# Sum of reciprocals over rows of 1024: loads of eight rows, chains of four, and a new split of additions and products

## The chip, the cores and the metric

The kernel runs on one core of a Trainium2 chip. The metric is the device time of one execution in microseconds (us), as a median of several runs. Beside it stands the profile of one execution: its span, from the first to the last instruction, and what each engine did in it. The engines are TensorE (PE in the profile), VectorE (DVE), ScalarE (ACT), GpSimd (POOL) and SyncE (SP), which here only issues transfers. There are also 16 DMA engines, which move the input from HBM into the on-chip memory SBUF. PSUM is a second, smaller on-chip memory, into which TensorE writes its results.

## The reference

```python
def setup_inputs():
    batch, seq, dim = 32, 512, 1024
    return {"x": np.abs(np.random.randn(batch, seq, dim)).astype(np.float32) + 1e-6}

def reference(x):
    return np.sum(1.0 / x, axis=-1).astype(np.float32)
```

The input is 67.1 MB, the output 64 KB. Every one of the 16384 rows of 1024 numbers becomes one number, the sum of its reciprocals.

## The kernel before

Each of the 128 partitions holds 128 rows of the input, so "a row" below means 128 x 1024 numbers, one row for each partition: 512 KB of input. The kernel goes through the 128 rows in 67 groups of one or two rows, in the list `GROUPS` (L39).

The arithmetic rests on 1/a + 1/b = (a + b) / (a b). A row is cut into halves a and b of 512 numbers (`H`). The product a b is needed for 512 places only, its reciprocal is taken by ACT as exp(-ln(S a b)) in two passes (`Ln`, L106, and `Exp`, L111), and DVE then multiplies with a + b and adds up the row, in one instruction with an accumulator (`tensor_tensor_reduce`, L118).

A group goes through these steps:

- SP issues its load (L83) into a tile `xt` of a pool with 16 buffers.
- POOL makes the products `pr` of its rows (L85); in the very last group DVE does.
- Where the group is marked `on_pe` (class B), TensorE adds the two halves of a row into a PSUM tile `sm`, as two matmuls with the identity matrix (L90). Each of these shows as two passes in the profile.
- ACT does `Ln` and `Exp` of the products. Without TensorE (class A) `Exp` writes to the PSUM tile `rc`, and with TensorE it writes back into `pr`.
- DVE sums the row. In class A it goes through all 1024 numbers of the row, each half against the same 512 reciprocals (`rc`); in class B through 512, `pr` against `sm`. In the profile the first is CUSTOM_DVE_ANT_1, the second CUSTOM_DVE_ANT_0, and a short read of the accumulator follows each.
- Class C has one row like class A and one that ACT does alone: `Ln` and `Exp` of all 1024 numbers with ACT's own accumulator (L98, L99).

The cycle is A, B, A, B, C, B, A, B, sixteen rows less one for POOL, seven times; then five groups of two rows, and six of one row. Each engine works through its instructions in the order of its queue and waits at each for what it needs. SP holds a load back until its buffer is free. At the end one transfer (L131) writes the sums out.

Of the kernel before, what the change touches and what calls it, by code (L numbers as in the profile page):

```python
# [1 line left out]

# [6 lines left out]


@with_exitstack
def kernel(
    ctx: ExitStack,
    tc: tile.TileContext,
    x: bass.AP,
    out: bass.AP,
):

    nc = tc.nc
    f32 = mybir.dt.float32
    P = 128
    D = 1024
    H = D // 2  # L30
    F = 128

    S = float(2**17)

    GP, DV = nc.gpsimd, nc.vector
    A, B, C = (2, 0, GP, False), (2, 0, GP, True), (1, 1, GP, False)
    GROUPS = (  # L39
        [A, B, A, B, C, B, A, B] * 7  # L40
        + [A, B, A, B, A]
        + [(1, 0, GP, True), (1, 0, GP, False)] * 2
        + [(1, 0, GP, True), (1, 0, DV, True)]
    )

    Ln = mybir.ActivationFunctionType.Ln
    Exp = mybir.ActivationFunctionType.Exp
    mult = mybir.AluOpType.mult
    add = mybir.AluOpType.add

    x_v = x.flatten_outer_dims().rearrange("(p f) d -> p f d", p=P)
    out_v = out.flatten().rearrange("(p f) -> p f", p=P)

    act_sets = list(get_activation_tables(nc.m.arch).keys())
    nc.scalar.add_instruction(  # L55
        mybir.InstLoadActFuncSet(
            name=nc.get_next_instruction_name(),
            act_func_set_id=act_sets.index("natural_log_exp_and_others"),
            ins=[],
            outs=[],  # L60
        )
    )

    xpool = ctx.enter_context(tc.tile_pool(name="xpool", bufs=16))
    ppool = ctx.enter_context(tc.tile_pool(name="ppool", bufs=4))
    opool = ctx.enter_context(tc.tile_pool(name="opool", bufs=1))
    rpool = ctx.enter_context(
        tc.tile_pool(name="rpool", bufs=2, space=bass.MemoryType.PSUM)
    )

    spool = ctx.enter_context(
        tc.tile_pool(name="spool", bufs=2, space=bass.MemoryType.PSUM)
    )

    sums = opool.tile([P, F], f32)
    ident = opool.tile([P, P], f32)
    make_identity(nc, ident)

    c0 = 0
    for np_, ns, eng, on_pe in GROUPS:  # L80
        n = np_ + ns
        xt = xpool.tile([P, n, D], f32, tag="xt")
        nc.sync.dma_start(out=xt, in_=x_v[:, c0 : c0 + n, :])  # L83
        pr = ppool.tile([P, np_, H], f32, tag="pr")
        eng.tensor_tensor(out=pr, in0=xt[:, :np_, :H], in1=xt[:, :np_, H:], op=mult)  # L85
        if on_pe:
            sm = spool.tile([P, np_, H], f32, tag="sm")
            for j in range(np_):
                for h in range(2):
                    nc.tensor.matmul(  # L90
                        sm[:, j, :],
                        lhsT=ident,
                        rhs=xt[:, j, h * H : (h + 1) * H],
                        start=h == 0,
                        stop=h == 1,
                    )
        for j in range(np_, n):
            nc.scalar.activation(out=xt[:, j, :], in_=xt[:, j, :], func=Ln)  # L98
            nc.scalar.activation(  # L99
                out=xt[:, j, :],  # L100
                in_=xt[:, j, :],
                func=Exp,
                scale=-1.0,
                accum_out=sums[:, c0 + j : c0 + j + 1],
            )
        nc.scalar.activation(out=pr, in_=pr, func=Ln, scale=S)  # L106
        if on_pe:
            rc = pr
        else:
            rc = rpool.tile([P, np_, H], f32, tag="rc")  # L110
        nc.scalar.activation(out=rc, in_=pr, func=Exp, scale=-1.0)  # L111
        for j in range(np_):
            if on_pe:
                row, rec = rc[:, j, :], sm[:, j, :]
            else:
                row = xt[:, j, :].rearrange("p (h e) -> p h e", h=2)
                rec = rc[:, j, :].unsqueeze(1).to_broadcast([P, 2, H])
            nc.vector.tensor_tensor_reduce(  # L118
                out=row,
                in0=row,  # L120
                in1=rec,
                scale=S,
                scalar=0.0,
                op0=mult,
                op1=add,
                accum_out=sums[:, c0 + j : c0 + j + 1],
            )
        c0 += n
    assert c0 == F, c0

    nc.sync.dma_start(out=out_v, in_=sums)  # L131


# [1 line left out]
_INS = ['x']  # L135
_OUTS = [((32, 512), 'float32')]


# [23 lines left out]
```

## Time and profile before

| | |
|---|---|
| median of 11 runs | 174.62 us (174.52 to 175.33) |
| profiled execution | 174.58 us, span 172.4 us |
| POOL busy | 143.4 us (83%) |
| ACT busy | 142.0 us (82%) |
| TensorE busy | 121.0 us (70%) |
| DVE busy | 109.8 us (64%) |
| DMA | 67.18 MB in the input queue, 390 GB/s over the span |

Times are microseconds from the start of the span. A busy share is an average over the whole span, so it doesn't say which engine sets the end; for that the stretches of time and the chain of waits are needed. In the groups of instructions, each row gives the source line, the engine, the operation and its tiles, how many there were, their busy time, the mean of one in ns, and behind the second bar how long the engine had stood idle before them and what ended that. "x" before a number counts instructions.

### The profile page before, as it was taken

What the parts mean: (1) busy time and instruction counts of PE and PEld (TensorE: products, weight loads), DVE (VectorE), ACT (ScalarE), POOL (GpSimd) and SP (SyncE); (2) the same over time, 40 slices, a digit from 0 to 9 for tenths busy, and PEclk for the clock granted to TensorE, in tenths of its full rate; (3) what the DMA queues carried; (4) which work ended last, traced back from release to release, by engine and by line L of the source; (5) the groups of instructions that cost most, each with busy time, mean ns of one, the idle gap of its engine ahead of it and who ended that gap; (6) DMA issues with size and microseconds to landing.
All of it is one profiled execution on the core that took longest, in us unless ns stands there. A gap on an engine that the chain in (4) does not pass through costs nothing.

```text
span 172.4 us, 1342 instructions
## 1 busy us (share of the span) xinstructions
PE 121.0 (70%) x256; PEld 47.4 (27%) x256; DVE 109.8 (64%) x243; ACT 142.0 (82%) x156; POOL 143.4 (83%) x72
## 2 busy tenths in 40 slices
PE   0099766666877667788676668976677877679480
PEld 0033322222332222233322223422222332223130
DVE  0009757874757757775578847577577755788791
ACT  2169989899878998889888997889888898988981
POOL 1698799969899799987999688996999879999920
PEclk9999999999999999999999996999999999999999
DMA  5999999999999999999999999999999999999500
GB/s 196 428 428 426 422 422 414 424 426 424 416 424 424 420 418 422 424 424 418 424 422 422 418 418 420 426 418 420 424 422 420 420 424 424 422 413 407 225 0 15
DMA packets 9799, 67.25 MB, mean 390 GB/s; under 512 B 1088, under 2 KB 1216, under 8 KB 1984
## 3 DMA queue, kind: packets, MB, share of 16 engines
q1 hardware_dynamic: 9792, 67.18, 94.0%
q8 instruction: 2, 0.03, 0.1%
q14 instruction: 5, 0.04, 0.1%
HBM read 67.11 MB, written 0.07 MB: 390 GB/s over the span
## 4 chain that ended last, share of the span: by engine, by line
DMA 78%; POOL 11%; ACT 2%; issue 2%; DVE 2%; SPq 2%; PE 1%; POOLq 0%; DVEq 0%
DMA xt<-in_x_dram 78%; POOL pr L85 11%; SPq L83 2%; ACT pr L106 1%; PE sm L90 1%; DVE xt L118 1%; ACT rc L111 1%; DVE pr L118 0%; ACT pr L111 0%; DVE pr L85 0%; POOLq L85 0%; DVE sums L118 0%; DVEq L118 0%; DVEq L157 0%
## 5 line engine op out<-in xcount | busy, mean ns | idle before, releaser
L85 POOL TENSOR_TENSOR pr<-xt 128x1024 f32<-128x1024 f32 (+1 forms) x66 | 142.7, 2167 | 20.8 <-DMA xt<-in_x_dram 16.5
L90 PE MATMUL sm<-xt,ident 128*128 128x512 f32 x256 | 121.0, 617 | 46.8 <-DMA xt<-in_x_dram 44.8
L118 DVE CUSTOM_DVE_ANT_1 xt<-xt,rc 128x1024 f32<-128x1024 f32 x57 | 67.7, 1218 | 50.3 <-issue 25.9
L106 ACT ACTIVATE pr<-pr 128x1024 f32<-128x1024 f32 (+1 forms) x67 | 65.0, 970 | 24.2 <-POOL pr L85 23.2
L90 PEld LDWEIGHTS sm<-xt,ident 128*128 128x128 f32 x256 | 47.4, 195 | 119.5 <-issue 62.0
L118 DVE CUSTOM_DVE_ANT_0 pr<-pr,sm 128x512 f32<-128x512 f32 x64 | 41.6, 685 | 9.5 <-ACT pr L111 8.2
L111 ACT ACTIVATE pr<-pr 128x1024 f32<-128x1024 f32 (+1 forms) x34 | 34.2, 1006 | 1.0
L111 ACT ACTIVATE rc<-pr 128x1024 f32<-128x1024 f32 (+1 forms) x33 | 29.9, 906 | 0.8
L118 DVE DVE_READ_ACCUMULATOR2_ANT sums<- 128x1 f32 x121 | 10.0, 82 | 0.0
L99 ACT ACTIVATE xt<-xt 128x1024 f32<-128x1024 f32 x7 | 7.3, 1041 | 0.0
L98 ACT ACTIVATE xt<-xt 128x1024 f32<-128x1024 f32 x7 | 7.3, 1040 | 0.0
L55 ACT ACT_TABLE_LOAD x1 | 1.3, 1283 | 0.7 <-PEq L146 0.7
L99 ACT ACTIVATION_READ_ACCUMULATOR xt<-xt 128x1 f32 x7 | 1.3, 187 | 0.0
L85 DVE TENSOR_TENSOR pr<-xt 128x512 f32<-128x512 f32 x1 | 0.7, 684 | 0.0
masks.py:197 POOL MEMSET ident<- 128x128 f32 x1 | 0.2, 205 | 0.3 <-POOLq L146 0.3
masks.py:199 POOL TENSOR_SCALAR_AFFINE_SELECT ident<-ident 128x128 f32<-128x128 f32 x1 | 0.3, 294 | 0.1
L146 POOL MEMSET const-float32-0.0<- 128x1 f32 x1 | 0.1, 99 | 0.2 <-issue 0.2
L146 POOL MEMSET const-bfloat16-1.0<- 128x1 bf16 x1 | 0.1, 102 | 0.0
L146 POOL MEMSET const-uint8-127<- 128x1 uint8 x1 | 0.1, 102 | 0.0
L146 POOL MEMSET const-float32-1.0<- 128x1 f32 x1 | 0.1, 99 | 0.0
## 6 DMA issues: line engine op xcount, KB each, us to landing
xt<-in_x_dram SPq DMA_DIRECT2D x61, 1024.0 KB, 19.8
xt<-in_x_dram SPq DMA_DIRECT2D x6, 512.0 KB, 15.6
out_dram<-sums SPq DMA_DIRECT2D x1, 64.0 KB, 1.5
```

Source lines behind the costliest of these rows:

```text
L55: nc.scalar.add_instruction(mybir.InstLoadActFuncSet(name=nc.get_next_instruction_name(), act_func_set_id=act_sets.index("natural_log_exp_ ...
L83: nc.sync.dma_start(out=xt, in_=x_v[:, c0 : c0 + n, :])
L85: eng.tensor_tensor(out=pr, in0=xt[:, :np_, :H], in1=xt[:, :np_, H:], op=mult)
L90: nc.tensor.matmul(sm[:, j, :], lhsT=ident, rhs=xt[:, j, h * H : (h + 1) * H], start=h == 0, stop=h == 1,)
L98: nc.scalar.activation(out=xt[:, j, :], in_=xt[:, j, :], func=Ln)
L99: nc.scalar.activation(out=xt[:, j, :], in_=xt[:, j, :], func=Exp, scale=-1.0, accum_out=sums[:, c0 + j : c0 + j + 1],)
L106: nc.scalar.activation(out=pr, in_=pr, func=Ln, scale=S)
L111: nc.scalar.activation(out=rc, in_=pr, func=Exp, scale=-1.0)
L118: nc.vector.tensor_tensor_reduce(out=row, in0=row, in1=rec, scale=S, scalar=0.0, op0=mult, op1=add, accum_out=sums[:, c0 + j : c0 + j + 1],)
L146: nc = _bacc.Bacc("TRN2", target_bir_lowering=False, num_devices=1)
```

## The change

The groups give way to 22 loads (`LOADS`): twelve of eight rows, then of 7, 6, 5, 4, 3, 2, 2, 1, 1 and 1. A load holds one or two chains of at most four rows, each given as (m, e, v): m rows, of which TensorE adds the halves of the first e, and DVE makes the products of the first v. An eight-row load is (4, 2, 0) and (4, 2, 1).

- A load of more than three rows uses one of four buffers of eight rows; the six small ones at the end have a buffer each (`epool`).
- POOL makes the products of up to four rows in one instruction. ACT takes `Ln` of a whole chain in one instruction, then `Exp` of the rows without TensorE into `rc` (two PSUM buffers), then `Exp` of the rows with TensorE in place. No row is done by ACT alone any more.
- TensorE writes each of its sums into a PSUM buffer of its own, of which there are four (before: two, of two rows each).
- For a row of which DVE makes the product, TensorE first copies half b into PSUM; DVE multiplies half a from SBUF with that copy; then TensorE adds half a. Only the last row (`DIRECT`) is multiplied from SBUF alone.
- DVE's sums of a chain (`sum_rows`) are put behind the products of the next chain (`waiting`). `keep` fixes the order of the loads, of POOL's and DVE's instructions and of the matmuls as written.

```diff
-    xpool = ctx.enter_context(tc.tile_pool(name="xpool", bufs=16))
+    xpool = ctx.enter_context(tc.tile_pool(name="xpool", bufs=4))
+    epool = ctx.enter_context(tc.tile_pool(name="epool", bufs=1))
...
+    LOADS = (
+        [[(4, 2, 0), (4, 2, 1)]] * 12
+        + [[(4, 2, 0), (3, 1, 1)], [(3, 1, 0), (3, 2, 1)], [(3, 1, 0), (2, 1, 1)]]
+        + [[(4, 2, 1)], [(3, 2, 1)], [(2, 1, 0)], [(2, 1, 1)]]
+        + [[(1, 0, 0)], [(1, 0, 0)], [(1, 1, 1)]]
+    )
+    DIRECT = 127
...
+    def add_half(s, half, start):
+        i = nc.tensor.matmul(
+            s, lhsT=ident, rhs=half, start=start, stop=True, skip_group_check=True
+        )
+        keep(i)
...
+    def sum_rows(c, xc, pr, sm, rc):
+        m, e = xc.shape[1], len(sm)
+        for j in range(e, m):
+            row = xc[:, j, :].rearrange("p (h e) -> p h e", h=2)
+            sum_row(c + j, row, rc[:, j - e, :].unsqueeze(1).to_broadcast([P, 2, H]))
+        for j in range(e):
+            sum_row(c + j, pr[:, j, :], sm[j])
...
+        for m, e, v in chunks:
+            xc = xt[:, q : q + m, :]
+            a, b = xc[:, :, :H], xc[:, :, H:]
+            pr = ppool.tile([P, m, H], f32, tag="pr")
+            sm = [spool.tile([P, H], f32, tag="s", name="s") for _ in range(e)]
+            if v < m:
+                keep(
+                    nc.gpsimd.tensor_tensor(
+                        out=pr[:, v:, :], in0=a[:, v:, :], in1=b[:, v:, :], op=mult
+                    )
+                )
+            for j in range(e):
+                add_half(sm[j], b[:, j, :], True)
+                if j >= v:
+                    add_half(sm[j], a[:, j, :], False)
+            for j in range(v):
+                other = b[:, j, :] if c0 + q + j >= DIRECT else sm[j]
+                keep(
+                    nc.vector.tensor_tensor(
+                        out=pr[:, j, :], in0=a[:, j, :], in1=other, op=mult
+                    )
+                )
+            for j in range(v):
+                add_half(sm[j], a[:, j, :], False)
+            if waiting:
+                sum_rows(*waiting)
+            nc.scalar.activation(out=pr, in_=pr, func=Ln, scale=S)
+            rc = None
+            if e < m:
+                rc = rpool.tile([P, m - e, H], f32, tag="rc")
+                nc.scalar.activation(out=rc, in_=pr[:, e:, :], func=Exp, scale=-1.0)
+            if e:
+                r = pr[:, :e, :]
+                nc.scalar.activation(out=r, in_=r, func=Exp, scale=-1.0)
+            waiting = c0 + q, xc, pr, sm, rc
+            q += m
```

`sum_row` is the same `tensor_tensor_reduce` as before, kept in order.

More of the change, by code (lines that the diff above doesn't have):

```diff
@@ L33 @@
     S = float(2**17)
[L37 to L43, printed above, removed]
+    LOADS = (
+        [[(4, 2, 0), (4, 2, 1)]] * 12
[3 rows of a table added]
     )
+    DIRECT = 127
     Ln = mybir.ActivationFunctionType.Ln
@@ L62 @@
     )
-    xpool = ctx.enter_context(tc.tile_pool(name="xpool", bufs=16))
+    xpool = ctx.enter_context(tc.tile_pool(name="xpool", bufs=4))
+    epool = ctx.enter_context(tc.tile_pool(name="epool", bufs=1))
     ppool = ctx.enter_context(tc.tile_pool(name="ppool", bufs=4))
     opool = ctx.enter_context(tc.tile_pool(name="opool", bufs=1))
+    spool = ctx.enter_context(
+        tc.tile_pool(name="spool", bufs=4, space=bass.MemoryType.PSUM)
+    )
     rpool = ctx.enter_context(
         tc.tile_pool(name="rpool", bufs=2, space=bass.MemoryType.PSUM)
-    )
-    spool = ctx.enter_context(
-        tc.tile_pool(name="spool", bufs=2, space=bass.MemoryType.PSUM)
     )
@@ L77 @@
     make_identity(nc, ident)
-    c0 = 0
[L80 to L95, printed above, removed]
-                    )
[L97 to L127, printed above, removed]
@@ new lines, with sum_row @@
+    keep = tc.keep_in_program_order
+    def add_half(s, half, start):
[3 more added lines that the diff above has]
+        keep(i)
+    def sum_row(c, row, fac):
+        i = nc.vector.tensor_tensor_reduce(
+            out=row,
+            in0=row,
+            in1=fac,
+            scale=S,
+            scalar=0.0,
+            op0=mult,
+            op1=add,
+            accum_out=sums[:, c : c + 1],
+        )
+        keep(i)
@@ new lines, in sum_rows @@
+    def sum_rows(c, xc, pr, sm, rc):
[5 more added lines that the diff above has]
+            sum_row(c + j, pr[:, j, :], sm[j])
+    waiting = None
+    c0 = 0
+    for k, chunks in enumerate(LOADS):
+        n = sum(m for m, _, _ in chunks)
+        if n > 3:
+            xt = xpool.tile([P, n, D], f32, tag="xt")
+        else:
+            xt = epool.tile([P, n, D], f32, tag=f"x{k}")
+        keep(nc.sync.dma_start(out=xt, in_=x_v[:, c0 : c0 + n, :]))
+        q = 0
+        for m, e, v in chunks:
[7 more added lines that the diff above has]
+                        out=pr[:, v:, :], in0=a[:, v:, :], in1=b[:, v:, :], op=mult
+                    )
+                )
[24 more added lines that the diff above has]
+            q += m
@@ L128 @@
         c0 += n
     assert c0 == F, c0
+    sum_rows(*waiting)
     nc.sync.dma_start(out=out_v, in_=sums)
```

## The prediction, made before the result was known

> **What bounds the kernel now.** The 40 slices come first (one character or number for 4.31 us).
>
> ```profile
> ACT  2169989899878998889888997889888898988981
> POOL 1698799969899799987999688996999879999920
> ...
> DMA  5999999999999999999999999999999999999500
> GB/s 196 428 428 426 422 422 414 424 426 424 416 424 424 420 418 422 424 424 418 424 422 422 418 418 420 426 418 420 424 422 420 420 424 424 422 413 407 225 0 15
> ```
>
> The DMA engines are full until about 160 us; then they stop while ACT and POOL go on. So the span is a full transfer plus a tail. The chain of waits, in order of time (start, us, what), shows where the tail is made:
>
> ```profile
> 118.98 19.81 DMA xt<-in_x_dram
> ...
> 138.95 2.35 POOL pr L85
> ...
> 156.29 2.39 POOL pr L85
> ...
> 158.70 1.06 ACT pr L106
> ...
> 168.85 0.69 DVE pr L118
> ```
>
> The chain follows DMA to 138.79, then POOL without a gap to 158.68, and only for the last 11 us a mixture of all engines. From 138.95 the timeline counts eight two-row and five one-row products on POOL, and DVE makes one: 22 rows, of which the first two landed at 138.79. So that was row 106 + 2 = 108 of 128. The first two had landed at 5.65 (POOL's first product begins at 5.75, after a wait for DMA). The **landing pace** is (138.79 - 5.65) / 106 = 1.256 us a row, which puts the last row at 138.79 + 20 x 1.256 = 163.9. The last sum ends at 169.55, the span at 172.4: 2.85 us for the output and the end.
>
> The groups by line and shape give prices (busy, mean ns of one | idle before):
>
> ```profile
> L85 POOL TENSOR_TENSOR pr<-xt 128x1024 f32<-128x1024 f32 x54 | 127.6, 2364 | 19.7 <-DMA xt<-in_x_dram 16.0
> L118 DVE CUSTOM_DVE_ANT_1 xt<-xt,rc 128x1024 f32<-128x1024 f32 x57 | 67.7, 1218 | 50.3 <-issue 25.9 <-ACT rc L111 12.7 <-POOL pr L85 11.8
> L118 DVE CUSTOM_DVE_ANT_0 pr<-pr,sm 128x512 f32<-128x512 f32 x64 | 41.6, 685 | 9.5 <-ACT pr L111 8.2
> ...
> L85 POOL TENSOR_TENSOR pr<-xt 128x512 f32<-128x512 f32 x12 | 15.2, 1278 | 1.1 <-DMA xt<-in_x_dram 0.6
> ```
>
> POOL: two rows 2.364, one 1.278, so 0.19 + 1.086 a row. A DVE sum from ACT's PSUM (ANT_1) and one with TensorE's sum (ANT_0) follow each other in the timeline every 1.145 and 0.605 us, the accumulator's read hidden. For ACT I take starts, since back-to-back instructions overlap (timeline of ACT):
>
> ```profile
> 158.70 1.06 ACT L106 ACTIVATE pr<-pr 128x1024 f32<-128x1024 f32 x1 [0.34 <-POOL pr L85]
> 159.79 1.03 ACT L111 ACTIVATE rc<-pr 128x1024 f32<-128x1024 f32 x1
> 160.75 0.61 ACT L106 ACTIVATE pr<-pr 128x512 f32<-128x512 f32 x1
> 161.40 0.63 ACT L111 ACTIVATE pr<-pr 128x512 f32<-128x512 f32 x1
> 161.93 0.61 ACT L106 ACTIVATE pr<-pr 128x512 f32<-128x512 f32 x1
> ```
>
> An Ln is followed by its own Exp after 1.09 us (two rows) or 0.65 (one); an Exp by the next instruction after 0.96 or 0.53. So Ln costs 0.21 + 0.44 a row, Exp 0.11 + 0.425 a row. From the same timeline: a POOL product reaches ACT after 0.03 us, an Exp in PSUM reaches DVE after 0.13, a DVE product reaches ACT after 0.04. DVE's one product of before (both inputs in SBUF) holds it for 0.61; with an input in PSUM, which no row shows, I take the same, as ANT_0 with such operands needs 0.605.
>
> [...] The four-row Ln, 2048 elements, no row shows; [...] The trace shows that: after a 2.13 us gap before 104.01 (columns: window, length, busy and count, granted clock, DMA share, GB/s)
>
> ```profile
> 101.00:104.00 3.00, 0.88 (x3) 1.00 1.03 421
> ...
> 105.00:106.00 1.00, 1.00 (x2) 0.50 1.05 442
> 106.00:107.00 1.00, 1.00 (x2) 0.50 1.01 418
> ...
> 109.00:110.00 1.00, 1.00 (x3) 1.00 1.03 426
> ```
>
> the passes took 0.85 us instead of 0.43.
>
> **The change, part by part.**
>
> *Loads of eight rows.* The same 67.1 MB come at, I assume, the same pace: 2-row loads already ran at 414 to 428 GB/s with 8 KB pieces. Larger pieces could gain something (rival 3). The first load lands at 5.65 + 6 x 1.256 = 13.2, 7.5 us later than now. What hides that: POOL's remaining work is 109 rows, 109 x 1.086 + 36 instructions x 0.28 (start and gap) = 128 us, and ends by 142 if unhindered; the transfers last until 163.9. Four 8-row buffers: in steady state a load is done 15.3 us after landing (POOL 4.67, ACT 3.89 twice, DVE's last sums 2.8), while the three behind it need 3 x 10.05 = 30.1 us to land. So SP has 15 us for reissuing, and the queue doesn't run dry. SP issues 22 loads instead of 67, at about 0.33 us each: nothing, behind full DMA.
>
> *Engines per eight rows (10.05 us of landing).* POOL 4 + 3 rows: 4.53 + 3.45 + 0.2 = 8.2, from 9.3 (a sixteen-row cycle of before: seven pairs and one single, 18.6). ACT 2 x (1.97 + 0.96 + 0.96) = 7.8. DVE 4 x 1.145 + 4 x 0.605 + one product 0.61 = 7.6. TensorE 8 x 0.86 = 6.9 at full clock. All are below 10.05: the first 96 rows cost nothing, whatever is removed there. ACT's own rows of class C go too, for the same reason free.
>
> *The tail.* The 7-row load lands at row 103: 138.79 - 5 x 1.256 = 132.5. POOL's four rows are done at 132.5 + 0.14 + 4.53 = 137.2, when ACT has long finished the load before (136.2). From there ACT has thirteen chains left, and smaller chains cost more a row: (4 rows) 3.89 twice, (3) 1.53 + 0.96 + 0.53 = 3.03 five times, (2) 1.09 + 2 x 0.53 = 2.16 three times, (1) 0.65 + 0.53 = 1.18 three times: **33.0 us**. Were there no gap, ACT would end at 170.2; that is already after now (168.82).
>
> *DVE's products.* Every product waits for TensorE's copy of half a row into PSUM (0.86 us); behind it in DVE's queue stand the previous chain's sums, ahead of it those of the one before that. ACT's Ln waits for it, and TensorE's second half, with the next chain's matmuls queued behind. In steady state it is ready 2.8 us before POOL's part. In the tail DVE is late. Following the thirteen chains with the prices above (start = the latest of engine, landing, predecessor, PSUM and pr buffers):
>
> ```
> rows left  chain    POOL done  product  ACT from-to      sums done
> 25         4 rows   137.2      -        137.2-141.1      143.9
> 22         3, v1    139.6      140.4    141.1-144.1      146.8
> 19         3        143.6      -        144.1-147.1      150.3
> 16         3, v1    146.1      147.4    147.5-150.5      152.7
> 13         3        149.9      -        150.5-153.5      156.2
> 11         2, v1    151.3      153.3    153.5-155.7      158.6
> 7          4, v1    154.9      156.8    156.8-160.7      163.6
> 4          3, v1    157.6      159.5    160.7-163.7      165.9
> 2 and 0:
>            2        160.1      -        163.7-165.9      168.4
>            2, v1    161.6      166.6    166.6-168.8      170.3
>            1        164.9      -        168.8-170.0      171.5
>            1        167.3      -        170.0-171.2      173.2
>            1, v1    -          172.1    172.1-173.3      174.1
> ```
>
> The gaps in ACT: 0.32 + 1.16 + 0.73 + 0.92 = **3.1 us**. Each arises alike: for the 4-row chain the sums of two chains earlier end at 156.2, the product takes 0.61, while ACT was free at 155.7. The last product multiplies straight from SBUF, but waits in DVE's queue all the same. POOL's late starts at the end (a pr buffer four chains back) end before ACT needs them. So: 170.2 + 3.1 + last sum and read 0.8 = 174.1; + 2.85 = span **176.9**. The profiled execution took 174.58 for a span of 172.4, 2.18 outside: 176.9 + 2.18 = **179.1 us**, 2.6% over the median of 174.62 (which the profiled one matches). Ends for what isn't shown: the gaps 0 to 5 us, the landing pace -3% to +1% of 132 us (-4 to +1)[...].
>
> **Rivals.** *1: products in time.* If DVE's sums are shorter or the order kinder, no gaps: 179.1 - 3.1 = 176.0. For: DVE is busy only 64% now. Against: the table, where ACT and DVE run neck and neck. *2: TensorE at half clock.* Eight rows leave it idle for 10.05 - 6.9 = 3.1 us a load, mostly in one piece, longer than the 2.13 that slowed it once. A slowed pass costs 0.43 more, four to eight such passes 1.7 to 3.4 us; in steady state ACT's 2.3 us of slack per load covers one, but in the tail PSUM sums and products come later by it: gaps grow by 1 to 3, 180 to 182. Against: TensorE becomes steadier busy when slowed. *3, on the faster side: pieces of 32 KB lift the transfer.* [...] It decides from 101 x d = 4.5 us, a pace of 1.211 (433 GB/s). Against: no 4.3 us slice of the profile exceeds 428. *4: the queue runs dry*, if a load is released more than 15 us later than I have it; each us late delays a landing by one, so 5 us late gives 184. I see nothing that would do it.
>
> **How the numbers follow.** The table's case 0.57, rival 1 0.15, rival 2 0.17, rival 3 0.08 (three quarters of it beyond parity), rival 4 0.03. A measurement of this kernel tells about 0.2% from no change (0.35 us). Rival 3 gives faster 0.06 and part of same 0.03; the rest, 0.91, is slower. The likeliest is 179.1, its own range 177.5 to 180.5. The range takes in rivals 1 and 2: 175.6 to 181.8, leaving out rivals 3 and 4 and the ends of 2.
>
> **What would show it.** Right: DMA still ends near 163.5; ACT nearly without gaps from 137 on, its waits there for DVE products, and the last Exp near 173; POOL done well before ACT. First wait of POOL about 13 us. Wrong: DMA well above 424 GB/s (rival 3), DMA gaps (4), TensorE at 0.5 clock in the tail (2), ACT's tail in one piece (1), or four-row Ln far from 1.9 us.

## The result, and the profile after

The changed kernel takes **176.97 us** (median of 13 runs, 175.9 to 177.95) beside 174.73 us for the kernel before: a ratio of 1.0105, with a 95% interval of 1.0087 to 1.0123, so it is slower. The runs of the kernel before fall into two groups, near 174.6 and near 175.4, and its median lies in the lower one; the quotient of the means (176.79 and 174.95) is 1.0105, that of the medians 1.013. The profiled execution took 176.01 us with a span of 174.2, so it is one of the shorter ones. Times here and below are those of undisturbed executions: one of e2 (179.34 us) and one of the kernel before (691.18 us, in the group of e5 to e8) are left out.

The 40 slices of the changed kernel (one of 4.36 us each):

```profile
DVE  0000396783989696987949698786959899998993
ACT  2000884957797795959498695959598998979962
POOL 1009859595978959594987959595989999795500
...
DMA  6999999999999999999999999999999999995000
GB/s 218 429 436 391 429 429 436 436 436 429 429 438 429 436 421 436 444 418 414 429 436 438 406 459 414 446 429 410 434 436 438 409 426 410 421 411 236 0 0 15
```

DMA moves more in most slices than the 414 to 428 GB/s of before, and stops some 2.6 us earlier (36.5 slices of 4.36 us against 37.5 of 4.31). ACT and POOL now show a hole in every load, and DVE, which was the least busy of the three before, is nearly full through the last ten.

POOL's timeline shows where loads land, since POOL waits for each of them (start, us, what, idle before and what ended it):

```profile
13.36 7.91 POOL L126 TENSOR_TENSOR pr<-xt 128x2048 f32<-128x2048 f32 x2 [12.06 <-DMA xt<-in_x_dram]
...
43.34 8.00 POOL L126 TENSOR_TENSOR pr<-xt 128x2048 f32<-128x2048 f32 x2 [1.77 <-DMA xt<-in_x_dram]
53.05 7.96 POOL L126 TENSOR_TENSOR pr<-xt 128x2048 f32<-128x2048 f32 x2 [1.71 <-DMA xt<-in_x_dram]
...
130.23 6.90 POOL L126 TENSOR_TENSOR pr<-xt 128x2048 f32<-128x2048 f32 x2 [0.54 <-DMA xt<-in_x_dram]
```

Two eight-row loads follow each other at 53.05 - 43.34 = 9.71 us, 1.214 us a row. The seven-row load lets POOL start at 130.23; the forecast had it land at 132.5. From the first load (row 8) to this one (row 103) the mean pace is (130.23 - 13.36) / 95 = 1.230 us a row, where the forecast had 1.256.

ACT's timeline of the last 32 rows, only those Ln that had to wait:

```profile
134.83 1.91 ACT L145 ACTIVATE pr<-pr 128x2048 f32<-128x2048 f32 x1 [0.75 <-POOL pr L126]
...
145.22 1.48 ACT L145 ACTIVATE pr<-pr 128x1536 f32<-128x1536 f32 x1 [0.48 <-DVE pr L137]
...
154.56 1.91 ACT L145 ACTIVATE pr<-pr 128x2048 f32<-128x2048 f32 x1 [1.14 <-DVE pr L137]
...
164.30 1.06 ACT L145 ACTIVATE pr<-pr 128x1024 f32<-128x1024 f32 x1 [0.17 <-DVE pr L137]
...
169.75 0.63 ACT L145 ACTIVATE pr<-pr 128x512 f32<-128x512 f32 x1 [1.54 <-DVE pr L137]
```

ACT begins the tail at 134.83 and then has gaps of 0.48, 1.14, 0.17 and 1.54 us, all waiting for a product of DVE. And the windows of the tail (engine busy, with the number of instructions: PE, PEld, DVE, ACT, POOL; then granted clock, DMA share, GB/s):

```profile
134.00:146.00 12.00, 9.91 (x22) 3.65 (x21) 11.39 (x25) 10.68 (x11) 11.31 (x5) 1.00 1.00 424
146.00:158.00 12.00, 10.12 (x23) 3.85 (x22) 11.23 (x26) 10.73 (x12) 10.55 (x5) 1.00 0.99 412
158.00:172.00 14.00, 6.79 (x15) 2.30 (x13) 13.44 (x30) 11.18 (x16) 3.84 (x3) 0.94 0.10 39
```

DVE, the third of them, is busy 11.39 + 11.23 + 13.44 = 36.1 of 38 us; ACT only 32.6, with the same list of work as in the forecast. In the same windows of the kernel before DVE had 26.0:

```profile
134.00:146.00 12.00, 9.42 (x21) 3.85 (x22) 7.09 (x18) 11.19 (x13) 10.44 (x5) 1.00 1.01 421
146.00:158.00 12.00, 9.30 (x21) 3.55 (x20) 9.39 (x19) 10.15 (x10) 11.44 (x6) 1.00 1.01 416
158.00:172.00 14.00, 7.22 (x16) 2.41 (x14) 9.49 (x23) 9.49 (x15) 6.82 (x6) 1.00 0.30 117
```

The chain of waits, in order of time:

```profile
112.04 4.53 POOL pr L126
116.58 1.92 ACT pr L145
118.53 1.04 ACT rc L149
...
122.73 6.21 PE s L83 x10
128.97 0.36 DVE pr L137
...
149.76 0.60 DVE pr L89
...
150.37 0.43 DVE pr L137
...
169.75 0.64 ACT pr L145
170.41 0.64 ACT pr L152
171.07 0.69 DVE pr L89
```

It leaves the transfer at 112 us and passes POOL and ACT once. From 119.70 it consists mainly of DVE's sums and products, until 137 us with TensorE's work between them (122.73: ten passes in 6.21 us, after an idle stretch of 2.18 us, with a granted clock of 0.50 from 123 to 125 us and 0.73 from there to 127); ACT stands in it for 3 us from 154.56, for 3.7 us from 164.30 and for the last row.

### The profile page after: what moved, and what is told of

It reads as the page before. It is cut to its first block, busy times and chain, and to the rows that moved or that the text cites. A ratio compares the mean times of both kernels' runs of the same rounds, so it can differ in the third digit from the quotient of the medians.

```text
span 174.2 us, 1180 instructions
## 1 busy us (share of the span) xinstructions
PE 123.8 (71%) x252; PEld 48.3 (28%) x252; DVE 127.1 (73%) x275; ACT 126.5 (73%) x109; POOL 125.7 (72%) x42
## 3 DMA queue, kind: packets, MB, share of 16 engines
q1 hardware_dynamic: 3312, 67.18, 90.7%
## 4 chain that ended last, share of the span: by engine, by line
DMA 41%; DVE 20%; ACT 11%; PE 11%; POOL 8%; issue 7%; SPq 0%; DVEq 0%; POOLq 0%; ACTq 0%
DMA xt<-in_x_dram 41%; DVE xt L89 13%; PE s L83 11%; POOL pr L126 8%; ACT pr L145 7%; DVE pr L89 4%; ACT rc L149 3%; DVE pr L137 2%; ACT pr L152 1%; DVE sums L89 1%; SPq L117 0%; POOLq L126 0%; DVEq L89 0%; DVEq L137 0%; ACTq L145 0%
## 5 line engine op out<-in xcount | busy, mean ns | idle before, releaser
L83 PE MATMUL s<-xt,ident 128*128 128x512 f32 x252 | 123.8, 639 | 43.4 <-DVE sums L89 24.5
L126 POOL TENSOR_TENSOR pr<-xt 128x1536 f32<-128x1536 f32 (+3 forms) x36 | 125.0, 3492 | 38.8 <-DMA xt<-in_x_dram 32.9
L145 ACT ACTIVATE pr<-pr 128x2048 f32<-128x2048 f32 (+3 forms) x37 | 61.9, 1672 | 42.6 <-POOL pr L126 38.5
L89 DVE CUSTOM_DVE_ANT_1 xt<-xt,rc 128x1024 f32<-128x1024 f32 x65 | 77.0, 1217 | 11.9 <-ACT rc L149 11.7
L83 PEld LDWEIGHTS s<-xt,ident 128*128 128x128 f32 x252 | 48.3, 202 | 118.0 <-issue 61.2
L89 DVE CUSTOM_DVE_ANT_0 pr<-pr,s 128x512 f32<-128x512 f32 x63 | 40.9, 682 | 0.2 <-ACT pr L152 0.2
L137 DVE TENSOR_TENSOR pr<-xt,s 128x512 f32<-128x512 f32 x18 | 12.3, 686 | 32.5 <-PE s L83 32.5
L149 ACT ACTIVATE rc<-pr 128x1024 f32<-128x1024 f32 (+1 forms) x36 | 34.0, 945 | 1.1
L152 ACT ACTIVATE pr<-pr 128x1024 f32<-128x1024 f32 (+1 forms) x35 | 33.4, 955 | 0.0
L89 DVE DVE_READ_ACCUMULATOR2_ANT sums<- 128x1 f32 x128 | 10.5, 82 | 0.0
```

The costliest lines, as they stand in the source:

```text
L83: i = nc.tensor.matmul(s, lhsT=ident, rhs=half, start=start, stop=True, skip_group_check=True)
L89: i = nc.vector.tensor_tensor_reduce(out=row, in0=row, in1=fac, scale=S, scalar=0.0, op0=mult, op1=add, accum_out=sums[:, c : c + 1],)
L126: nc.gpsimd.tensor_tensor(out=pr[:, v:, :], in0=a[:, v:, :], in1=b[:, v:, :], op=mult)
L137: nc.vector.tensor_tensor(out=pr[:, j, :], in0=a[:, j, :], in1=other, op=mult)
L149: nc.scalar.activation(out=rc, in_=pr[:, e:, :], func=Exp, scale=-1.0)
L152: nc.scalar.activation(out=r, in_=r, func=Exp, scale=-1.0)
```

## The experiments

The profile suggests these theories, named by letters. For the transfer: **P**, a DMA engine pays a fixed time per piece of contiguous bytes, and pieces are now 32 KB instead of 8 KB; against **D**, more bytes are in flight. For the tail: **V**, DVE's work is the bound; against **A**, ACT's 33 us of chains are, with some gaps added. The runs of a group share a chip and its runs of the kernel before.

### e1 and e4: the changed kernel with smaller transfers

```diff
-        keep(nc.sync.dma_start(out=xt, in_=x_v[:, c0 : c0 + n, :]))
+        for r in reversed(range(0, n, 2)):      # e4: 4
+            w = min(2, n - r)
+            keep(nc.sync.dma_start(out=xt[:, r : r + w, :],
+                                   in_=x_v[:, c0 + r : c0 + r + w, :]))
```

Two-row pieces. Expected:

> The changed kernel with every load cut into transfers of two rows (8 KB a partition) into the same tile, last rows first, so that no chain starts earlier. Theory P (a transfer costs a DMA engine a fixed time per piece of contiguous bytes; from the two profiles, 162.1 us in packets with 8 KB pieces and 158.0 with 32 KB, about 0.011 us a piece and 0.0382 us a KB): DMA time per engine back to 162, a row lands every 1.25 us instead of 1.215, and the time rises by 2 to 3 us over 177.0, to about 179.3. Theory D (the transfer gained because more bytes are in flight, not because of the pieces): with eight transfers of 1 MB in flight also slower, so this run alone doesn't tell D from P. Theory N (the pace differs by chance of the execution): 177.0.

Measured: 179.39 us (178.67 to 180.88), ratio to before 1.0263 (1.0199 to 1.0328). POOL's timeline of e1:

```profile
33.11 7.95 POOL L132 TENSOR_TENSOR pr<-xt 128x2048 f32<-128x2048 f32 x2 [2.00 <-DMA xt<-in_x_dram]
43.05 7.96 POOL L132 TENSOR_TENSOR pr<-xt 128x2048 f32<-128x2048 f32 x2 [1.99 <-DMA xt<-in_x_dram]
...
133.16 6.89 POOL L132 TENSOR_TENSOR pr<-xt 128x2048 f32<-128x2048 f32 x2 [0.90 <-DMA xt<-in_x_dram]
```

Eight rows now need 9.94 us, and the seven-row load lets POOL start 2.9 us later than in the changed kernel. (The tail of this execution is another 1.0 us longer, 42.5 us from POOL's start to the last sum instead of 41.5; DVE waits in it for TensorE for 0.87 and 1.00 us, and the granted clock is 0.86 from 146 to 158 us.)

Four-row pieces. Expected:

> As the run with two-row pieces, but transfers of at most four rows (16 KB pieces). Theory P: 0.011 + 16 x 0.0382 = 0.622 us a piece, 159.3 us per engine, pace 1.225, time 0.5 to 1 us over the changed kernel's 177.0: 177.7. Theory D: buffers and bytes in flight as in the changed kernel, so 177.0 and DMA time 158.

Measured: 178.26 us (177.01 to 179.54), ratio 1.0212 (1.0137 to 1.0287). POOL's timeline of e4:

```profile
43.76 7.95 POOL L132 TENSOR_TENSOR pr<-xt 128x2048 f32<-128x2048 f32 x2 [1.83 <-DMA xt<-in_x_dram]
53.54 7.97 POOL L132 TENSOR_TENSOR pr<-xt 128x2048 f32<-128x2048 f32 x2 [1.83 <-DMA xt<-in_x_dram]
```

Loads follow at 53.54 - 43.76 = 9.78 us. The changed kernel's page has 3312 packets in the input queue: 22 loads of 128 pieces, and 496 packets under 2 KB. Eight rows are 128 partitions of 32 KB, of which each of the 16 engines moves 8 if they share evenly (an estimate), in 32, 16 or 8 pieces. So 9.94 - 9.78 = 0.16 us for 16 pieces, and 9.78 - 9.71 = 0.07 us for 8: about **0.01 us a piece** either way, as P has it. The time that the packets took on each engine agrees with P's forecasts of 162 and 159.3: 91.0% of 178.3 = 162.3 us in e1 and 91.0% of 175.2 = 159.4 in e4, beside 90.7% of 174.2 = 158.0 in the changed kernel. One rival stays open: in all these runs every transfer has just eight pieces for each engine, so a fixed time per transfer, of 0.07 to 0.08 us by the same two differences, would look the same. No run separates piece and transfer. The time of e4 scatters too much to decide anything by itself.

### e2: three large buffers instead of four

```diff
-    xpool = ctx.enter_context(tc.tile_pool(name="xpool", bufs=4))
+    xpool = ctx.enter_context(tc.tile_pool(name="xpool", bufs=3))
```

> The changed kernel with three buffers of eight rows instead of four: some 6 MB in flight instead of 10. Theory P (pieces): DMA time per engine stays at 158, pace 1.215, time 176.0 to 178.0 as the changed kernel. Theory D (bytes in flight): pace 1.25 or worse, time 179 or more. Theory Q (the queue was close to running dry): gaps in DMA, first before the fifth load, and 180 or more.

Measured: 176.84 us (176.63 to 177.78), ratio 1.0121 (1.0072 to 1.0169), as the changed kernel. Its loads land every 9.71 us too (82.15, then 91.86), with less in flight; D falls. Its slices hold something else:

```profile
DMA  6999999999999999999999999999998878999200
GB/s 225 427 427 412 442 435 420 442 435 427 450 407 450 435 420 439 420 442 435 412 450 414 450 427 414 450 412 420 446 405 382 306 308 307 427 424 409 116 0 15
```

In slices 31 to 34 the queue does run dry, where the loads shrink and a buffer of eight rows holds five; about a quarter of three slices is lost (306 to 308 GB/s). The time doesn't show it: from 137 us on DVE, which needs what lands then, stands idle for 0.61, 0.52, 0.33, 0.59 and 0.22 us only.

### e3: loads of eight rows in the kernel before

```diff
-        xt = xpool.tile([P, n, D], f32, tag="xt")
-        nc.sync.dma_start(out=xt, in_=x_v[:, c0 : c0 + n, :])
+        if c0 >= 112:
+            xt = epool.tile([P, n, D], f32, tag="xs")
+            nc.sync.dma_start(out=xt, in_=x_v[:, c0 : c0 + n, :])
+        else:
+            if c0 % 8 == 0:
+                big = xpool.tile([P, 8, D], f32, tag="xt")
+                nc.sync.dma_start(out=big, in_=x_v[:, c0 : c0 + 8, :])
+            xt = big[:, c0 % 8 : c0 % 8 + n, :]
```

> The kernel before, with its own groups, engines and order, but the first 112 rows loaded eight at a time (four buffers), the last sixteen rows in its own loads of two and one. Theory P: rows up to 112 land every 1.215 us, the last row near 160.5 instead of 163.9. If POOL's backlog sets the end (my reading of the chain), POOL has row 112 done about 9.4 us after it landed at 140, near 150, needs 19 us more, and the span is 169 + 7.6 = about 176.5, the time 178.5: slower than before although the data come sooner. If the transfer sets the end, 174.6 - 3.4 = 171.2.

Measured: 177.79 us (177.32 to 178.26), ratio 1.0161 (1.0124 to 1.0197). POOL's end:

```profile
141.69 1.27 POOL L92 TENSOR_TENSOR pr<-big 128x512 f32<-128x512 f32 x1 [0.38 <-DMA big<-in_x_dram]
143.40 7.03 POOL L92 TENSOR_TENSOR pr<-big 128x1024 f32<-128x1024 f32 x3 [0.43 <-ACT rc L118]
150.39 17.85 POOL L92 TENSOR_TENSOR pr<-xt 128x1024 f32<-128x1024 f32 x10
```

Row 112 is there sooner (141.6 us; at the pace of before it would come at 138.79 + 4 x 1.256 = 143.8), but POOL has done the rows of this last large load only 9 us after they landed, and from 150.39 it works 17.85 us without a gap, to 168.24; before it ended at 164.83. Large loads alone cost this kernel 1.6%: at the end a large load is a large lag for POOL.

### e11, e5 and e6: ACT or DVE in the tail

e5 and e6 hold ACT in program order (`keep` around its three instructions), so that the planner, which orders what `keep` leaves free, can't rearrange it. e11 is that alone:

> The changed kernel with nothing but ACT held in program order, the common base of e5, e6 and e7. The planner had moved one single-row Ln ahead in a gap of 0.65 us near the end. If that matters, 0.5 us slower, 177.5; if not, 177.0.

Measured: 177.23 us (176.75 to 178.18), ratio 1.013 (1.0082 to 1.0178): no difference that these runs can tell. It is the base for the next three.

```diff
-            if e:
+            if e and c0 + q < 96:      # e5: no Exp in place for the last 32 rows
                 r = pr[:, :e, :]
```

> The changed kernel with ACT held in program order, and without the second Exp (that of the rows with TensorE's sum) for the last 32 rows: four of two rows and seven of one, 4 x 0.96 + 7 x 0.53 = 7.6 us less for ACT. It leaves out the reciprocals of those 15 rows; DVE and all others do what they did. Theory A (ACT's 33 us of chains set the tail, the gaps are added to it): 4 to 7 us faster than the changed kernel's 177.0, 170 to 173. Theory V (DVE sets the tail: it is busy 36.1 of the 38 us from 134 to 172, and ACT's gaps are DVE's work seen from ACT): within 1 us of 177.0.

Measured: 176.52 us (175.7 to 177.23), ratio 1.0084 (1.0056 to 1.0113). The windows of e5:

```profile
134.00:146.00 12.00, 9.89 (x22) 3.47 (x20) 11.20 (x25) 8.98 (x8) 11.31 (x5) 1.00 0.99 422
146.00:158.00 12.00, 10.00 (x22) 3.96 (x23) 11.67 (x26) 8.65 (x8) 11.44 (x5) 1.00 0.99 411
158.00:172.00 14.00, 7.73 (x17) 2.68 (x15) 13.38 (x30) 8.63 (x12) 3.83 (x3) 1.00 0.12 49
```

ACT has lost 33.4 - 26.3 = 7.1 us of work in this stretch against e11, DVE is as full as there (36.3 and 36.2 us), and the time is 0.7 us under e11, less than either scatters. In the profiled executions the tail from ACT's Ln of the seven-row load to the last sum is as long as before: 36.7 us (135.75 to 172.45), beside 37.0 in e11. A falls: ACT's chains are not what sets the tail.

```diff
-        + [[(4, 2, 0), (3, 1, 1)], [(3, 1, 0), (3, 2, 1)], [(3, 1, 0), (2, 1, 1)]]
-        + [[(4, 2, 1)], [(3, 2, 1)], [(2, 1, 0)], [(2, 1, 1)]]
+        + [[(4, 2, 0), (3, 1, 1)], [(3, 1, 0), (3, 2, 1)], [(3, 1, 0), (2, 1, 0)]]
+        + [[(4, 2, 0)], [(3, 2, 0)], [(2, 1, 0)], [(2, 1, 0)]]
```

> The changed kernel with ACT in program order and the four DVE products of the chains with 11, 7, 4 and 0-to-2 rows left (not the last row's) given to POOL: DVE loses 4 x 0.61 = 2.4 us in the tail, ACT nothing, POOL gains 4 x 1.09 to 1.28. Theory V: about 2.4 us faster, 174.5. Theory A: only the gaps at those chains go (1.14 + 0.17 us), 175.7. Theory P2 (POOL, which then ends later, takes over): 176 or more, with ACT waiting for POOL.

Measured: 175.12 us (174.5 to 175.65), ratio 1.0006 (0.9992 to 1.0021): four products of 0.61 us less on DVE, and 2.1 us less than e11. The windows:

```profile
146.00:158.00 12.00, 11.47 (x26) 4.21 (x24) 10.02 (x23) 11.31 (x12) 12.00 (x5) 1.00 0.99 411
158.00:172.00 14.00, 5.42 (x12) 2.20 (x12) 12.43 (x29) 10.86 (x16) 6.78 (x4) 0.91 0.12 45
```

DVE has room now (10.02 of 12 us), and POOL is full in its place. This undoes the whole loss against the kernel before. The tail of the profiled executions is shorter by 1.4 us (35.6 instead of 37.0), less than DVE's 2.4, as ACT now waits 0.56 us for POOL and DVE stands idle for 0.50 and 1.47 us (in the changed kernel it was 0.33 and 0.44). So the size of e6's gain, between V's 174.5 and A's 175.7, doesn't tell V from A by itself; e5 does.

### e7: DVE's products from SBUF alone

```diff
-    DIRECT = 127
+    DIRECT = 0
```

Theory S is that DVE's products and POOL's, when both read SBUF, hold each other up. It was an assumption of mine, which no trace had shown.

> The changed kernel with ACT in program order and every DVE product taken from SBUF alone (DIRECT = 0), so that no product waits for TensorE's copy; 18 products change. Theory W (the copy into PSUM only costs a wait): DVE's 32.5 us of waiting for TensorE go, most of it in the first 96 rows where it is covered; the tail gains under 1 us, and the runs scatter less: 175.7 to 176.5. Theory S [...]: products take up to 4.5 us in the trace, or POOL's grow by 0.6, and the tail loses 1 to 4 us: 178 or more.

Measured: 180.16 us (179.6 to 181.31), ratio 1.0297 (1.0232 to 1.0362). The groups of e7, and then of the changed kernel:

```profile
L126 POOL TENSOR_TENSOR pr<-xt 128x2048 f32<-128x2048 f32 x13 | 59.6, 4586 | 34.0 <-DMA xt<-in_x_dram 31.8 <-DVE sums L89 1.7 <-DVE pr L137 0.5
...
L137 DVE TENSOR_TENSOR pr<-xt 128x512 f32<-128x512 f32 x19 | 40.1, 2112 | 13.4 <-DMA xt<-in_x_dram 13.4
```

```profile
L126 POOL TENSOR_TENSOR pr<-xt 128x2048 f32<-128x2048 f32 x13 | 59.1, 4547 | 33.4 <-DMA xt<-in_x_dram 31.0 <-ACT pr L145 2.4
...
L137 DVE TENSOR_TENSOR pr<-xt,s 128x512 f32<-128x512 f32 x18 | 12.3, 686 | 32.5 <-PE s L83 32.5
```

A product takes 2.11 us in the mean instead of 0.69, up to 3.57, while POOL's instruction grows only from 4.55 to 4.59 us: DVE is the one held most. POOL's short instructions near the end are held too: one row takes 1.56 us instead of 1.28, two rows 2.58 instead of 2.38. So the copy through PSUM is worth 2.9 us here (180.16 against 177.23), although it makes every product wait for TensorE.

### e8, e9, e12 and e10: chains that leave DVE room

e8 replaces the loads: four rows each, ten buffers of four, and a tail in which DVE makes the product of the last row only. ACT is in program order in all four.

```diff
+        [[(4, 2, 0)], [(4, 2, 1)]] * 12
+        + [[(3, 2, 0)]] * 9
+        + [[(2, 1, 0)]] * 2
+        + [[(1, 1, 1)]]
```

> A version meant to beat both: loads of four rows (ten buffers of four), the first 96 rows in the changed kernel's chains, then nine loads of three rows with two on TensorE, two of two with one, and one row; no DVE products in the tail but the last. Against the changed kernel's tail DVE has 32 x 0.605 + 12 x 0.54 = 25.8 + 0.6 us for sums and product instead of 36, and the lag at row 96 is one chain less. Theory V: DVE no longer sets the end; landing (16 KB pieces, 1.224 us a row, the last row near 161) plus POOL, ACT and DVE of the last chains does: 172 to 173.5. Theory A: ACT has 9 x 3.0 + 2 x 2.15 + 1.2 = 32.5 us, much as before, and begins some 3 us earlier: 174.

Measured: 173.71 us (173.18 to 175.28), ratio 0.9929 (0.99 to 0.9958), faster than both kernels. The windows:

```profile
134.00:146.00 12.00, 12.00 (x30) 5.30 (x29) 8.75 (x24) 10.20 (x10) 11.34 (x4) 1.00 1.01 426
146.00:158.00 12.00, 12.00 (x30) 5.30 (x29) 7.34 (x18) 10.07 (x12) 11.32 (x4) 1.00 1.01 423
158.00:172.00 14.00, 7.66 (x18) 2.80 (x16) 9.60 (x23) 9.44 (x12) 6.13 (x3) 0.95 0.19 74
```

DVE is at 8.75, 7.34 and 9.60 us, and the chain of waits follows the transfer again, from 128.65 to 155.87, before it passes to POOL (from 156.03) and ACT. TensorE, which adds more rows here (21 of the last 32 instead of 15), is now the full engine, with 12.00 of 12 us twice.

Two runs ask whether e8 gained by its loads or by its tail; both take e8's four-row loads with the changed kernel's tail. e9 had two buffers for the loads of seven, six and five rows:

> Which half of the version with small chains made the gain: here its loads of four rows for the first 96 rows, but the changed kernel's own chains for the last 32 (ACT in program order). Theory V (DVE's work in the tail is the bound, and DVE is busy without a gap from about row 96 on): the earlier landing of half the rows helps little, since DVE also pays for the smaller pieces' slower pace (1.224): 176 to 177.5. Theory L (the lag of an 8-row load at row 96 is what made the changed kernel late): 174.

Measured: 185.81 us (185.57 to 186.3), ratio 1.0622 (1.0578 to 1.0667). It tells nothing of the question; its DMA row shows why:

```profile
DMA  6999999999999999999999999999950299999000
```

The five-row load waited for the release of the seven-row one, and the queue stood nearly or half empty for three slices of 4.6 us (253, 4 and 85 GB/s, some 10 us of transfer lost). It did measure the forecast's fourth rival. e12 gives each large load a buffer:

> As e9, but with a buffer of its own for each of the loads of seven, six and five rows (five of four rows for the rest), so that the 5-row load needn't wait for the release of the 7-row one, which in e9 left the DMA engines without work for some 16 us. Theory V (DVE's work in the tail is the bound): 176 to 177.5, no gain over the changed kernel from the smaller loads alone. Theory L (the lag of an 8-row load at row 96 made the changed kernel late): 174.

Measured: 177.11 us (177.04 to 177.61), ratio 1.0142 (1.0114 to 1.017), as the changed kernel. Here ACT and DVE had caught up before the seven-row load: ACT stood idle for 5.93 us until that load's products came at 135.69, DVE for 5.84 us until 138.35. Yet the end came as late, the last sum at 172.7 against 171.8, and from POOL's start on the seven-row load (131.14) to there it took as long as in the changed kernel: 41.6 and 41.5 us. So it isn't a lag from row 96 that sets the end; it is when the seven-row load lands, and the last 32 rows' work from there on. The gain of e8 lies in its tail, where the loads are smaller (three rows at first instead of seven) and the chains leave DVE more room; these two were not tried apart.

e10 has e8's code, with a tail chosen by the same sum as in the forecast:

```diff
-        + [[(3, 2, 0)]] * 9
-        + [[(2, 1, 0)]] * 2
-        + [[(1, 1, 1)]]
+        + [[(4, 2, 0)], [(2, 1, 1)], [(2, 1, 0)], [(3, 3, 1)], [(3, 2, 0)], [(1, 0, 0)]]
+        + [[(2, 0, 0)], [(3, 3, 1)], [(2, 0, 0)], [(3, 2, 1)]]
+        + [[(2, 1, 0)], [(2, 1, 0)], [(2, 2, 0)], [(1, 1, 1)]]
```

> The version with small chains (e8) with another tail, chosen so that by the measured prices no engine has to wait long: more rows with TensorE, three chains with a DVE product, loads of 1 to 4 rows. The same sum that gave 172.7 for e8 (measured 173.7) gives 171.2 here: 172.2 if the sum is right but for the same 1.0, 173.7 or more if the new products wait as they did in the changed kernel.

Measured: **172.72 us** (172.02 to 172.89), ratio 0.9854 (0.9808 to 0.9901), the fastest of all: 1.5% under the kernel before and 4.2 us under the changed one.

```profile
134.00:146.00 12.00, 9.82 (x23) 4.20 (x24) 9.21 (x21) 10.95 (x12) 10.46 (x6) 1.00 1.00 418
146.00:158.00 12.00, 11.14 (x26) 4.22 (x25) 11.03 (x25) 10.97 (x12) 9.96 (x5) 1.00 1.01 425
158.00:172.00 14.00, 8.87 (x21) 3.53 (x19) 9.98 (x25) 9.59 (x13) 5.66 (x3) 0.99 0.20 80
```

No engine is full in any of the three windows: DVE 30.2 us of 38, ACT 31.5. Which of the differences from e8 brings the 1.0 us (TensorE relieved, smaller loads, a product in three chains) was not tried apart.

## Why the prediction was right and wrong

The direction was right and so were the lengths in the tail; the size was not: 2.6% slower was forecast, about 1% was measured. The 176.97 us lie within 175.6 to 181.8, but below the 177.5 to 180.5 that the forecast gave its likeliest case. By the steps of the sum:

- **"The same 67.1 MB come at, I assume, the same pace": wrong.** This is the step that failed. The mean pace was 1.230 us a row instead of 1.256, and over 95 rows that brought the seven-row load 2.4 us before its forecast. The cause is the size of the transfers and their pieces: eight rows took 9.94 us in 8 KB pieces and 9.71 in 32 KB pieces (e1 against the changed kernel). The forecast let the pace vary by -3% to +1% at the ends of its range, but put the gain at nothing in its sum. Rival 3 pointed the right way, but I gave it only 0.08, an estimate with no trace behind it, and took it to decide from 433 GB/s on, where each of 101 rows lands d = 0.045 us sooner. 9.71 us for 4.19 MB is 432, but two intervals of 10.4 us (from 13.36 and from 72.48) pulled the mean down to 426. I had no slice above 428 and took that for a limit; with pieces of 8 KB again no slice of e1 exceeds 430, but in the changed kernel single ones reach 459. With these put back (e1) the forecast of 179.1 meets 179.39, in part by luck: the executions of e1 spread from 178.67 to 180.88, and the profiled one has that longer tail.
- **ACT's 33.0 us: right.** From 134.83 to 171.04, less 3.33 us of gaps, are 32.9. From one start to the next a four-row Ln took 1.95 us against 1.97 (134.83 to 136.78), and POOL's four rows took 4.55 against 4.53. No row of before has four rows in one instruction, or a product of DVE while POOL works: that these prices would stay was an estimate, and it held.
- **Gaps of 3.1 us from DVE's products: right in size** (3.33) and in three of four places (0.48, 1.14 and 1.54 for 0.32, 1.16 and 0.92). At the third of the four the planner moved a one-row Ln into the gap and left 0.17 of the 0.73; what ACT didn't wait there it waited at the end. (The column "rows left" of the forecast's table doesn't count the last three single rows, and POOL's 9.3 us for eight rows of before are 8.9 by its own prices; neither enters the sum.) **How I named it was wrong**: I wrote 33 us of ACT plus gaps, as if the gaps were an addition that better products would remove. The gaps are DVE's list seen from ACT. DVE needs 17 x 1.145 + 15 x 0.605 + 7 x 0.61 = 32.8 us for the last 32 rows, as much as ACT, and starts some 3 us after it. e5 shows the difference: 7.6 us less for ACT bring at most 0.7.
- **The rest of the sum**: from the last sum to the end of the span were 2.4 us instead of 2.85 (171.77 to 174.2), and outside the span 1.8 instead of 2.18. Why these two differ from before isn't known. In the profiled execution the terms are 2.4 + 0.4 + 0.4 us below the forecast, less 0.2 for the gaps: 3.0, against 179.1 - 176.0 = 3.1. The median is 1 us above the profiled execution; what made the others longer isn't known.
- **The first 96 rows cost nothing: right.** POOL waits for DMA at nearly every load, and e12 changes its loads without effect.
- **Rival 1** (no gaps) can't be had from ACT's side, as e5 shows; e6 is its real form. **Rival 2** was partly true: reduced clock shows in several slices, in the chain at 122.73 and in the tail of e1 (0.86 from 146 to 158 us). An idle stretch alone doesn't tell when: in the changed kernel the passes after 2.96, 2.15 and 2.18 us (at 34.54, 63.78 and 122.73) came to a granted clock of 0.50, those after 2.85 us (at 93.60) ran at 1.00. The times scatter as well: runs of the changed kernel by 2 us, those of e6 by 1.1. That the clock is what scatters them was not tested. **Rival 4** did not happen in the changed kernel; e9 showed its price, 9 us for a queue that stood empty or half empty for some 10.

## What to carry to other kernels

When a kernel streams from HBM, price the transfer by the size of its loads and pieces too: "no slice above 428" was what loads of two rows had shown, and here eight rows took 9.94 us in 8 KB pieces and 9.71 in 32 KB. Write the tail as a list for every engine, not only for the one that looks last, and ask of each gap whose work it is: a gap in one engine that is filled by another's list went here only as that other list got shorter (2.4 us off DVE's list brought 2.1 in e6, 7.1 off ACT's brought 0.7 in e5). And a saving in the part that is covered by the transfer bought nothing by itself (in e12 ACT and DVE stood idle for over 5.8 us before the seven-row load, and the time was 177.11 us beside 176.97); four products moved from DVE to POOL in the last sixteen rows were worth as much as the whole loss.

## What the runs showed of the hardware

- Larger transfers with longer contiguous pieces came faster: eight rows (256 KB an engine) took 9.94, 9.78 and 9.71 us as four, two transfers or one, in pieces of 8, 16 and 32 KB. That is about 10 ns a piece or 0.07 to 0.08 us a transfer; the runs don't tell which. Three large buffers instead of four made no difference to the pace (9.71 us, e2).
- A VectorE product with two SBUF inputs took up to 3.57 us beside GpSimd's products (mean 2.11, in e7) and 0.69 with one input in PSUM (in the changed kernel). It was mostly VectorE that was held: GpSimd's products of four rows grew from 4.55 to 4.59 us, those of one row from 1.28 to 1.56.
- Now and then a load was held up: POOL's starts lay 10.4 us apart instead of 9.71 at two places in the changed kernel's execution, and up to 10.9 and 11.1 in those of e1 and e4. No cause was found.
